# Attention probabilities and differential outputs turned by VectorE and DMA instead of TensorE

## The chip, the cores and the metric

One core of a Trainium2 chip runs the whole kernel. The metric is the device time of one execution in microseconds (us). The kernel before has a median of 2001.21 us over 3 runs (2001.2 to 2002.17). Matmuls run on TensorE (PE in the profile; PEld is its loading of the stationary operand), elementwise work on VectorE (DVE) and ScalarE (ACT). SyncE (SP) issues DMAs, and so does GpSimd (POOL), which does little else here.

## What is computed

Two transformer blocks on 256 tokens of width 2048, in float32. The first is sliding-window attention with sinks (called branch A here), 32 heads of 64:

```
scores = einsum('bnqhgd,bnkhd->bnhgqk', q, kb) * HEAD_DIM ** -0.5 - slopes * dist
p = softmax(concat([where(valid, scores, NEG), sink_col]))[..., :-1]
o = einsum('bnhgqk,bnkhd->bnqhgd', p, vb)
x = x + rmsnorm((o * silu(z)) @ w_out, g_post)
```

The second runs two attentions on the same normed input and merges them with gates, and ends with a feed-forward layer:

```
# latent branch, 16 heads of 128 + 64 rope
p = softmax(where(chunk_allowed, (qn @ kn.T + qr @ kr.T) * scale, NEG));  y_mla = p @ v
# differential branch, 8 heads, each with two maps of 128 and values of 256
a = softmax(s0) - lam * softmax(s1);  y_diff = rmsnorm_2(a @ v, sub_g) * (1 - lambda_init)
x = x + (g0 * (y_mla @ w_mla) + g1 * (y_diff @ w_diff)) @ w_out
h = rmsnorm_2(x);  x = x + (silu(h @ w_gate) * (h @ w_up)) @ w_down
out = rmsnorm_2(x)
```

With tokens in two blocks of 128, one head's probabilities are three 128x128 squares: the first query block sees one key block, the second sees two. They lie in a tile of 128 partitions (queries) by 384 columns (keys). To multiply them with the values, keys have to lie on the partitions, so each square has to be transposed.

## The kernel before

**Weights.** All weight matrices are cut on the host into 5440 tiles of 128x128, in the order in which the kernel takes them, sixteen to a chunk of 1 MB. `Weights.load` issues one DMA for a chunk on SP, into one of four `w_raw` tiles. `Weights.cut` splits half a chunk at a time into a rounded part `w_hi` (ACT, L85) and the rest `w_lo` (DVE, L86), each with four buffers; matmuls take both parts, so that their sum has float32's precision. A load waits until the chunk four before it has been cut, a cut until PE is done with the half four before it. SP's queue is in order, so whatever stands in it ahead of a load holds the load up.

**What runs between the weights.** `gemm`, `gemm_nat` and their relatives stream the weights through PE, and call `between.tiles` as they go. Every `between.every` tiles (8 or 5 in attention) that is a tick of an `Interleave`, which lets one piece of other work be written into the program there. A piece is a generator; the number that it yields is the count of ticks until its next step. In this way the attention of earlier columns stands between the weight matmuls of later ones. `attention_a` is the generator of branch A, `attend_m` that of a pair of latent heads, `attend_d` that of a differential head, `turn_residual` that of the residual after the first block.

**Turning.** `transposed` (L437) makes three PE transposes against an identity into a PSUM bank of tag `t` and copies the bank to SBUF, on DVE or ACT. In branch A the scores of pair i are followed a tick later by the transposes of pair i-1, and the values of pair i-2 stand just ahead of the scores of pair i. `attend_m` yields once before its transposes and once after them; `attend_d` transposes its probabilities at L883, splits them out of PSUM into `a_hi` and `a_lo`, multiplies, scales by the reciprocal root mean square that POOL computes (`rstd`, L280), and transposes the output at L907.

The feed-forward layers and the residual are turned in another way: DVE's `transpose` turns each 32x32 block in place, and `moved` (L449) sends the sixteen quarters, 32 partitions by 128 columns each, to where they belong, by sixteen small DMAs on POOL's queue (on SP's for two tiles of the output projection). `turn_residual` sends its eight tiles, 128 moves, on POOL.

**Memory.** Nearly all SBUF tiles are units of 128 partitions by 512 float32, in one pool of 67.

## Time and profile before

| | |
|---|---|
| median of 3 runs | 2001.21 us |
| the profiled execution | 2001.22 us, of which the span on the core is 1999.4 us |
| mean granted TensorE clock | 0.998 |
| instructions in the span | 26446 |
| read from HBM | 364.03 MB, 183 GB/s over the span |

The span is what the profile shows, from the first to the last instruction; the 1.8 us around it are in the time alone. Branch A runs from about 50 to 230 us, the latent branch from about 440 to 580, the differential heads and the residual between 600 and 1040, and the rest is merging and the feed-forward layer. Rows of groups give line, engine, operation, output and inputs, shapes, count, then busy time and mean length of one, and the engine's idle time just before them with what ended it. DVE and VectorE, ACT and ScalarE, POOL and GpSimd are the same engines; SPq and POOLq are their queues of DMA issues and waits.

### The profile page before, as it was taken

To read this page: it belongs to the slowest core of one execution; us is meant where nothing else is said; L and a number is where in the kernel's file an instruction comes from. 1 tells how busy PE (TensorE), PEld (TensorE's weight loads), DVE (VectorE), ACT (ScalarE), POOL (GpSimd) and SP (SyncE) were. 2 spreads that over 40 slices of the span, in tenths; PEclk is the share of its full clock that TensorE was granted. 3 is DMA by queue.
4 is the path that set the end of the run, shared out by engine and by line. 5 is a ranking of instruction groups with operands and counts; after the bars stand their busy time and mean duration, and the time that the engine had idled before them with its cause. 6 is when DMAs were issued, how large, how long until landed. Compare 5 with 4: busy or idle time off the path is not lost.

```text
span 1999.4 us, 26446 instructions
## 1 busy us (share of the span) xinstructions
PE 1982.0 (99%) x9956; PEld 1670.1 (84%) x9956; DVE 1231.3 (62%) x1892; ACT 1011.4 (51%) x1585; POOL 366.5 (18%) x737
## 2 busy tenths in 40 slices
PE   9999999999999999999999999999999999999997
PEld 8888888888888888888888888888888888888886
DVE  7778766977866555576565566655555555544553
ACT  6777655756545444455454344544444444434443
POOL 0000000000000542100000475533434333330000
PEclk9999999999999999999999999999999999999999
DMA  8444455444444655545555665655655655565552
GB/s 302 152 148 148 163 199 196 148 150 156 146 168 169 218 209 198 196 166 188 175 185 215 213 219 191 236 200 211 208 208 204 203 208 209 203 221 191 194 198 90
DMA packets 78512, 379.95 MB, mean 190 GB/s; under 512 B 18032, under 2 KB 30832, under 8 KB 35248
## 3 DMA queue, kind: packets, MB, share of 16 engines
q1 hardware_dynamic: 53664, 361.31, 50.8%
q0 software_dynamic: 23568, 14.99, 2.6%
q10 hardware_dynamic: 1152, 1.97, 0.3%
q8 instruction: 78, 1.28, 0.3%
q14 instruction: 50, 0.41, 0.1%
HBM read 364.03 MB, written 2.10 MB: 183 GB/s over the span
## 4 chain that ended last, share of the span: by engine, by line
PE 96%; DVE 2%; ACT 1%; issue 1%; POOL 0%; POOLq 0%; ACTq 0%
PE ps_g L199 90%; PE ps_s L199 4%; PE ps_t L199 2%; PE ps_t L441 1%; DVE rope_t L202 1%; DVE w_lo L86 0%; DVE k_n L202 0%; PE ps_warm L220 0%; DVE q_r L202 0%; ACT w_hi L85 0%; PE ps_t L907 0%; ACT prob L432 0%; PE ps_t L883 0%; DVE prob L426 0%; DVE y_m L236 0%
## 5 line engine op out<-in xcount | busy, mean ns | idle before, releaser
L86 DVE TENSOR_TENSOR w_lo<-w_raw,w_hi 128x1024 fp32r<-128x1024 f32 (+1 forms) x677 | 823.8, 1219 | 599.0 <-ACT w_hi L85 588.8
L85 ACT CAST w_hi<-w_raw 128x1024 fp32r<-128x1024 f32 (+1 forms) x677 | 710.0, 1051 | 727.0 <-PE ps_g L199 683.0
L199 PE MATMUL ps_g<-w_hi,t_hi 128*128 128x512 f32 x1176 | 457.5, 389 | 0.0
L199 PE MATMUL ps_g<-w_lo,t_hi 128*128 128x512 f32 x1176 | 457.5, 389 | 0.0
L199 PE MATMUL ps_g<-w_hi,t_lo 128*128 128x512 f32 x1176 | 457.3, 389 | 0.0
L454 POOL DMA_DIRECT2D turned<-turn x576 | 282.6, 498 | 453.8 <-DVE turn L461 251.7
L199 PE MATMUL ps_g<-h,w_hi 128*128 128x512 f32 x1160 | 284.7, 394 | 0.0
L199 PEld LDWEIGHTS ps_g<-w_lo,t_hi 128*128 128x128 f32 x1176 | 220.7, 188 | 45.9
L199 PEld LDWEIGHTS ps_g<-w_hi,t_lo 128*128 128x128 f32 x1176 | 220.7, 188 | 45.8
L199 PEld LDWEIGHTS ps_g<-w_hi,t_hi 128*128 128x128 f32 x1176 | 220.7, 188 | 45.8
L199 PEld LDWEIGHTS ps_g<-h,w_hi 128*128 128x128 f32 x1160 | 211.9, 188 | 44.1 <-issue 3.5
L199 PE MATMUL ps_g<-w_hi,h 128*128 128x512 f32 x768 | 241.3, 391 | 0.0
L199 PEld LDWEIGHTS ps_g<-w_hi,h 128*128 128x128 f32 x768 | 144.2, 188 | 29.9
L199 PE MATMUL ps_g<-h,w_lo 128*128 128x256 f32 x1160 | 156.3, 285 | 0.0
L199 PEld LDWEIGHTS ps_g<-h,w_lo 128*128 128x128 f32 x1160 | 148.9, 191 | 8.5 <-issue 3.2
L199 PE MATMUL ps_g<-w_lo,h 128*128 128x512 f32 x384 | 149.5, 389 | 0.0
L280 POOL TENSOR_TENSOR rstd<-ms,mhalf 128x2 f32<-128x2 f32 x14 | 12.4, 886 | 666.7 <-DVE ms L275 649.1
L199 PEld LDWEIGHTS ps_g<-w_lo,h 128*128 128x128 f32 x384 | 72.1, 188 | 14.7
L454 POOL DMA_DIRECT2D x1n<-turn x128 | 62.9, 499 | 103.0 <-DVE turn L936 86.7
L199 PE MATMUL ps_g<-w_hi,y_m 128*128 128x512 f32 x256 | 80.0, 390 | 0.0
L199 PE MATMUL ps_g<-w_hi,y_d 128*128 128x512 f32 x256 | 79.0, 389 | 0.0
L199 PE MATMUL ps_g<-g,w_hi 128*128 128x512 f32 (+1 forms) x240 | 57.8, 377 | 0.0
(244 smaller groups left out, 1780.5 us busy)
## 6 DMA issues: line engine op xcount, KB each, us to landing
w_raw<-w SPq DMA_DIRECT2D x337, 1024.0 KB, 4.8
turned<-turn POOLq DMA_DIRECT2D x576, 16.0 KB, 3.9
row<-rw POOLq DMA_DIRECT2D x12, 256.0 KB, 4.4
w_raw<-w SPq DMA_DIRECT2D x5, 512.0 KB, 7.5
x1n<-turn POOLq DMA_DIRECT2D x128, 16.0 KB, 3.9
x_t<-xt SPq DMA_DIRECT2D x7, 256.0 KB, 7.5
row<-rw SPq DMA_DIRECT2D x4, 256.0 KB, 6.1
out<-x1n SPq DMA_DIRECT2D x4, 256.0 KB, 3.2
```

Source lines behind the costliest of these rows:

```text
L85: a = nc.scalar.copy(out=hi[:, q], in_=src[:, q])
L86: b = nc.vector.tensor_tensor(out=lo[:, q], in0=src[:, q], in1=hi.bitcast(F32)[:, q], op=ALU.subtract)
L199: nc.tensor.matmul(out=o, lhsT=a, rhs=b, start=start, stop=stop, skip_group_check=True)
L202: nc.vector.tensor_tensor(out=o, in0=a, in1=b, op=op)
L280: nc.gpsimd.tensor_tensor(out=r, in0=t, in1=mhalf[:, 0:n], op=ALU.pow)
L441: nc.tensor.transpose(out=ps[:, j * P:j * P + P], in_=p[:, j * P:j * P + P], identity=ident)
L454: queue.dma_start(out=o[32 * b:32 * b + 32, a * P:a * P + P], in_=tr[32 * a:32 * a + 32, b * P:b * P + P])
```

## The change

Three turns go from PE to DVE and DMA.

1. The probabilities of the two heads of a pair (branch A, latent branch), or of two differential heads, are turned together by the new `turned_probs`: two DVE block transposes into a wide tile of 128 by 768 columns, then sixteen moves of 32 partitions by 192 columns, twelve on POOL's queue and four on SP's, into a second wide tile. The wide tiles come from a pool of their own with six buffers. The value matmuls read the turned tile in place, as runs of 32 columns.
2. The outputs of the differential heads are copied out of PSUM, scaled, turned by DVE (`turned_values`), moved by sixteen DMAs on POOL, and split in pieces of 128 columns. `attend_d` now takes two heads at a time, with one `rstd` for both.
3. The residual's 128 moves go from POOL's queue to SP's.

The steps stand further apart: values of branch A follow three pairs after scores instead of two, `attend_m` yields 4 and 13 ticks, `attend_d` 9 and 8. The unit pool has 57 buffers instead of 67; after the last attention the wide pool is closed, and eight units of the feed-forward activations lie in its place.

```diff
-    def transposed(p, on_act=False):
-        ps = bank("t")
-        for j in range(3):
-            nc.tensor.transpose(out=ps[:, j * P:j * P + P], in_=p[:, j * P:j * P + P], identity=ident)
...
+    def moved(tr, o, queue=nc.gpsimd, fourth=None):
+        n = tr.shape[-1] // 4
         for a in range(4):
             for b in range(4):
+                (fourth if fourth and a == 3 else queue).dma_start(
+                    out=o[32 * b:32 * b + 32, a * n:a * n + n], in_=tr[32 * a:32 * a + 32, b * n:b * n + n])
...
+    def turned_probs(p):
+        tr = wide("prob_tr")
+        o = tr.rearrange("p (b e k i) -> p e k b i", b=4, e=2, k=3)
+        for e in range(2):
+            nc.vector.transpose(out=o[:, e], in_=p[e].rearrange("p (k b i) -> p k b i", k=3, b=4))
+        d = moved(tr, wide("prob_t"), fourth=nc.sync).rearrange("p (a e k i) -> p e k a i", a=4, e=2, k=3)
+        return [d[:, e] for e in range(2)]
...
-            mm(ps[64 * e:64 * e + 64, 0:S], vs[2 * e], pts[e][:, 0:S], True, False)
+            mm(ps[64 * e:64 * e + 64, 0:S], vs[2 * e], pts[e][:, 0:2], True, False)
...
     def attention_a():
-        p, pts = {}, {}
-        for i in range(18):
+        pts = {}
+        for i in range(19):
             while i < 16 and i >= len(q_o):
                 yield
-            if i >= 2:
-                values_a(i - 2, pts.pop(i - 2))
+            if i >= 3:
+                values_a(i - 3, pts.pop(i - 3))
             if i < 16:
-                p[i] = scores_a(i)
-            yield 1
-            if 0 < i < 17:
-                a, b = p.pop(i - 1)
-                pts[i - 1] = [transposed(a), transposed(b, True)]
-            yield 2
+                p = scores_a(i)
+                yield 2
+                pts[i] = turned_probs(p)
+                yield 1
+            else:
+                yield 3
...
-        yield
-        pts = [transposed(p[e], e == 1) for e in range(2)]
-        yield
+        yield 4
+        pts = turned_probs(p)
+        yield 13
...
+    def turned_values(o, r):
+        tr = unit("o_tr")
+        to = tr.rearrange("p (b d q i) -> p q d b i", b=4, d=2, q=2)
+        for qb in range(2):
+            nc.vector.tensor_scalar(out=half(o, qb), in0=half(o, qb), scalar1=r[:, qb:qb + 1], scalar2=None,
+                                    op0=ALU.mult)
+            nc.vector.transpose(out=to[:, qb], in_=half(o, qb).rearrange("p (d b j) -> p d b j", d=2, b=4))
+        return moved(tr, unit("o_t"))
+
+    def attend_d(u, q, k, v):
+        heads = (2 * u, 2 * u + 1)
+        p = []
+        for e, head in enumerate(heads):
+            p.append(probs_d(head, q[e], k[e]))
+            yield
+        pts = turned_probs(p)
+        yield 9
+        ms = sm("ms_d")
+        os = []
+        for e in range(2):
+            os.append(values_d(pts[e], [(half(a, e), half(b, e)) for a, b in v], ms[:, 2 * e:2 * e + 2]))
+            yield
         r = rstd(ms, S)
         yield
+        ots = [turned_values(o, r[:, 2 * e:2 * e + 2]) for e, o in enumerate(os)]
+        for e, head in enumerate(heads):
+            yield 8
...
-                x1n.append(moved(tr, "x1n"))
+                x1n.append(moved(tr, unit("x1n"), nc.sync))
...
-NU = 67
+NU = 57
```

The order of PE's instructions in branch A, before, from the values of one pair through its neighbours' scores to the next transposes (`ps_t`, `ps_s`, `ps_g` are PSUM banks of the tags t, s and g; `h` numbered are parts of the normed input; rows of weight matmuls between are cut at both ends):

```order
L199 MATMUL ps_g<-h_202,w_lo 128x256
L199 MATMUL ps_t<-prob_t,v_a 64x256 x2
L199 MATMUL ps_t<-prob_t,v_a 64x128 x2
L199 MATMUL ps_s<-k_a,q_a 128x128 x2
L199 MATMUL ps_s<-k_a,q_a 128x256 x2
```

and sixteen rows of weight matmuls on:

```order
L199 MATMUL ps_g<-h_292,w_hi 128x512
L199 MATMUL ps_g<-h_321,w_hi 128x512
L199 MATMUL ps_g<-h_324,w_hi 128x512
L441 MATMUL ps_t<-ident,prob 128x128 x6
L199 MATMUL ps_g<-h_229,w_lo 128x256
L199 MATMUL ps_g<-h_232,w_lo 128x256
```

The same place of the changed kernel, with the semaphores that a row waits for in brackets (DMASW are those of POOL's DMAs, DMAHW of SP's):

```order
L209 MATMUL ps_g<-h_327,w_hi 128x512
L209 MATMUL ps_t<-prob_t,v_a 64x256 [waits DMASW6_49,DMASW5_49,DMASW7_49,DMASW4_49,DMAHW0_49,DMASW3_49,DMAHW1_49,DMASW2_49,DMAHW2_49,DMASW1_49,DMAHW7_49,DMASW0_49,PE_49]
L209 MATMUL ps_t<-prob_t,v_a 64x256
L209 MATMUL ps_t<-prob_t,v_a 64x128 x2
L209 MATMUL ps_s<-k_a,q_a 128x128 [waits DVE_49] x2
L209 MATMUL ps_s<-k_a,q_a 128x256 x2
```

The six transposes are gone, and the first value matmul of a pair waits for twelve DMA semaphores, eight of POOL's and four of SP's. On PE they take six wait instructions ahead of the matmul.

The order of SP's DMA issues before, from the start of the weight stream to the output projection (`w_raw` are the chunks):

```order
L54 DMA w_raw<-w 128x2048 x3
L515 DMA tab_a<-cst 128x384
L54 DMA w_raw<-w 128x2048 x174
L482 DMA row<-rw 128x512 x4
L54 DMA w_raw<-w 128x2048 x27
L454 DMA turned<-turn 32x128 x16
L54 DMA w_raw<-w 128x2048 x6
```

The changed kernel's, in the time of the residual and the first differential heads:

```order
L452 DMA x1n<-turn 32x128 x16
L54 DMA w_raw<-w 128x2048
L452 DMA x1n<-turn 32x128 x16
L54 DMA w_raw<-w 128x2048 x6
L452 DMA x1n<-turn 32x128 x32
L54 DMA w_raw<-w 128x2048 x7
L452 DMA x1n<-turn 32x128 x32
L54 DMA w_raw<-w 128x2048 x18
L452 DMA prob_t<-prob_tr 32x192 x4
L54 DMA w_raw<-w 128x2048 x13
```

Where 174 chunks followed each other, SP now issues moves between them: four at a time for probabilities, and the residual's in blocks of 16, twice two blocks together.

More of the change, by code (lines that the diff above doesn't have):

```diff
@@ L184, in unit, with wide, unit2 @@
         return up.tile([P, 512], dt, name=name, tag="u", bufs=NU)
+    def wide(name):
+        return wp.tile([P, 768], F32, name=name, tag="w", bufs=6)
+    def unit2(name, dt=F32):
+        return up2.tile([P, 512], dt, name=name, tag="u2", bufs=8)
     def sm(name, n=4):
@@ L461, in turned @@
         nc.vector.transpose(out=tr, in_=z)
-        return moved(tr, "turned", queue)
+        return moved(tr, unit("turned"), queue)
+    def turned_probs(p):
[5 more added lines that the diff above has]
+        return [d[:, e] for e in range(2)]
     def split_turned(acts, k0, parts):
@@ L879, in attend_d, with values_d @@
                                            in1=p[1][:, a:b], op0=ALU.mult, op1=ALU.add)
-        yield
-        ps = bank("t")
-        for j in range(3):
-            nc.tensor.transpose(out=ps[:, j * P:j * P + P], in_=p[0][:, j * P:j * P + P], identity=ident)
+        return p[0]
+    def values_d(pt, v, ms):
         ah, al = unit("a_hi", F32R)[:, 0:384], unit("a_lo", F32R)[:, 0:384]
-        nc.scalar.copy(out=ah, in_=ps[:, 0:384])
-        tt(al, ps[:, 0:384], ah.bitcast(F32), ALU.subtract)
-        yield
+        oh, ol = (o.rearrange("p (k a i) -> p k a i", k=3, a=4) for o in (ah, al))
+        nc.scalar.copy(out=oh, in_=pt)
+        tt(ol, pt, oh.bitcast(F32), ALU.subtract)
         ps = bank("t")
@@ L960, in block_kernel @@
             between.every, between.apart = 8, 3
-        for i in range(2):
-            between.add(attend_d(2 * u + i, qk[i], qk[2 + i], [(half(a, i), half(b, i)) for a, b in v]))
+        between.add(attend_d(u, qk[0:2], qk[2:4], v))
         if u == 0:
```

56 lines of the change are left out of this document (26 added, 30 removed).

## The prediction

> **What bounds the kernel now.** I read the page first: busy shares, slices, chain.
>
> ```profile
> PE 1982.0 (99%) x9956; PEld 1670.1 (84%) x9956; DVE 1231.3 (62%) x1892; ACT 1011.4 (51%) x1585; POOL 366.5 (18%) x737
> PE   9999999999999999999999999999999999999997
> PEclk9999999999999999999999999999999999999999
> PE 96%; DVE 2%; ACT 1%; issue 1%; POOL 0%; POOLq 0%; ACTq 0%
> ```
>
> PE is busy 99% of the span at the full granted clock, in every slice, and 96% of the chain that ended last is PE. So an instruction taken off PE shortens the run by its own time, as long as nothing else becomes late. Next the chain of waits in order of time, from 113 to 135 us (start, length, engine, tile, line, count), which is branch A:
>
> ```profile
> 113.92 3.88 PE ps_g L199 x16
> 117.80 0.66 PE ps_t L441 x6
> 118.46 5.56 PE ps_g L199 x32
> 124.02 0.80 PE ps_t L199 x8
> 124.82 0.85 PE ps_s L199 x8
> 125.67 2.10 PE ps_g L199 x16
> 127.78 0.66 PE ps_t L441 x6
> 128.43 5.59 PE ps_g L199 x32
> ...
> 134.02 0.80 PE ps_t L199 x8
> 134.82 0.86 PE ps_s L199 x8
> ```
>
> These pieces follow each other without a hole. Values (0.80) and scores (0.85) of a pair, weights, six transposes (0.66): two pairs take about 21.8 us (113.07 to 134.82, by the scores before and after), 10.9 a pair.
>
> **The transposes leave PE: -22.0.** The groups by form give their count:
>
> ```profile
> L441 PE MATMUL ps_t<-ident,prob 128*128 128x128 f32 x144 | 19.6, 272 | 0.6 <-DVE prob_t L446 0.6
> ...
> L907 PE MATMUL ps_t<-ident,o_d 128*128 128x128 f32 x32 | 4.8, 272 | 0.0
> ...
> L883 PE MATMUL ps_t<-ident,prob 128*128 128x128 f32 x24 | 3.9, 272 | 0.0
> ```
>
> 144 + 32 + 24 = 200. The mean of 272 ns overlaps with the next matmul; what one costs is 0.66 / 6 = 0.11 us by the chain. 200 x 0.11 = **22.0**. The other end is the busy time, 19.6 + 4.8 + 3.9 = 28.3, which counts pipeline tails; I take the chain. The 0.6 us at the end of the first row is PE waiting for a free transposing bank; it goes too: **-0.6**.
>
> [...]
>
> **Semaphores on PE: +4.3.** The order shows the first value matmul of a pair waiting for twelve DMA semaphores, where it waited for none of its own before. The built program puts them on six wait instructions in PE's queue, for 16 pairs of branch A and 8 of the latent branch (the differential heads wait on ACT and DVE instead). The one row with such an instruction on PE:
>
> ```profile
> L441 PEldq EVENT_SEMAPHORE  x10: 51/51/51, 60.4 to 560.4; - x10
> ```
>
> Six take 0.31 us at least; the time between two, no row shows. The queue may run ahead of the matmul in progress, which hides about one matmul: 3.88 / 16 = 0.24 or 2.10 / 16 = 0.13 us by the chain. That leaves 0.07 to 0.18 a pair. I take 0.18, since the six cannot take less than 0.31: 24 x 0.18 = **4.3**. Ends: 0, and 24 x 0.61 = 14.7 if each costs double and none is hidden.
>
> **DVE in branch A: +1.5.** DVE gives up a copy and gains two transposes:
>
> ```profile
> L446 DVE COPY prob_t<-ps_t 128x384 f32<-128x384 f32 x24 | 13.1, 548 | 0.4 <-PE ps_t L441 0.4
> ...
> L461 DVE STREAM_TRANSPOSE turn<-ffn 128x512 f32<-128x512 f32 x22 | 15.5, 703 | 0.0
> ...
> L936 DVE STREAM_TRANSPOSE turn<-y 128x128 f32<-128x128 f32 x32 | 8.0, 288 | 0.0
> ```
>
> 384 columns lie between: 288 + (703 - 288) x 256/384 = 565 ns. So 2 x 0.565 - 0.55 = +0.58 us a pair, plus its own wait instructions before it may overwrite a wide tile. Where gates overlap attention, DVE has little room (busy time by stretch: length, then PE, PEld, DVE, ACT, POOL):
>
> ```profile
> 150.00:200.00 50.00, 50.00 (x322) 41.38 (x320) 43.42 (x116) 38.30 (x99) 0.00 (x0) 1.00 0.43 148
> 200.00:250.00 50.00, 50.00 (x305) 42.36 (x304) 39.59 (x86) 32.68 (x72) 0.00 (x0) 1.00 0.45 164
> ```
>
> 43.42 / 50 x 10.9 = 9.5 us of DVE a pair; with 0.58 and some 0.3 of waits 10.4, and a pair now takes 10.9 - 0.66 + 0.18 = 10.4. DVE is full for five pairs. Ends 0 and 5 x 1.0; I take **1.5**. After 600 us DVE has 40% free, which hides what the differential heads add (two transposes of 565 ns and four of about 0.43 per two heads, and copies), and ACT loses its copies.
>
> **The quarters' way is hidden, and SP pays: +1.5.** POOL's moves of before (ns, least, median, most), and the DMA issues (count, size, us to landing):
>
> ```profile
> L454 POOL DMA_DIRECT2D turned<-turn x576: 496/498/550, 1119.7 to 1769.1; - x192
> ...
> w_raw<-w SPq DMA_DIRECT2D x337, 1024.0 KB, 4.8
> turned<-turn POOLq DMA_DIRECT2D x576, 16.0 KB, 3.9
> ...
> turned<-turn SPq DMA_DIRECT2D x32, 16.0 KB, 2.1
> ```
>
> And VectorE's timeline of one softmax, its first and its last step:
>
> ```profile
> 125.70 0.35 DVE L426 CUSTOM_DVE_ANT_0 prob<-ps_s,bias,negsink 128x128 f32<-128x128 f32 x1 [1.15 <-PE ps_s L199]
> ...
> 129.39 0.62 DVE L566 TENSOR_SCALAR prob<-prob,rec 128x256 f32<-128x256 f32 x2
> ```
>
> A pair's probabilities are ready at 130.0, 5.2 us after its scores (124.82). Then 1.1 of transposes, 12 x 0.498 = 6.0 of issue on POOL, 3.9 to land: 16.2 us. Values now come three pairs after scores, 3 x 10.4 = 31 us. SP's four moves can stand behind a weight load by one load interval (5.4): 8 us of cover stay. The latent branch waits 13 ticks of 5 weight tiles, the differential one 9 of 8, both above 20 us. If that cover were gone, PE would idle by each us, 24 times. So 0 here. The last heads' 32 moves take 16 + 3.9 us of the 8 ticks (22 us) that they have.
>
> SP also takes the residual's 128 moves, two times 32 in a row with no load between them, by the order. Rows for that: SP's timeline, PE's chain over the same time, and the two halves of a cut:
>
> ```profile
> 1228.15 10.96 SPq L54 DMA_DIRECT2D w_raw<-w  x3
> 1242.18 10.10 SPq L454 DMA_DIRECT2D turned<-turn  x16
> 1252.37 19.59 SPq L54 DMA_DIRECT2D w_raw<-w  x6
> ...
> 1037.82 943.88 PE ps_g L199 x4164
> ...
> L86 DVE TENSOR_TENSOR w_lo<-w_raw,w_hi 128x1024 fp32r<-128x1024 f32 (+1 forms) x677 | 823.8, 1219 | 599.0 <-ACT w_hi L85 588.8
> L85 ACT CAST w_hi<-w_raw 128x1024 fp32r<-128x1024 f32 (+1 forms) x677 | 710.0, 1051 | 727.0 <-PE ps_g L199 683.0
> ```
>
> Sixteen moves hold SP for 10.2 us; PE did not stop. A chunk is 24 matmuls of 943.88 / 4164 = 0.227, so 5.44 us. At a load's issue three chunks lie uncut (16.3) and four halves are cut (10.9, less 1.05 + 1.22 of cutting): PE needs the new chunk 24.9 us later. It needs 4.8 to land and 2.3 to be cut, so it can be 17.8 late; loads may lie 5.44 + 17.8 = 23.2 apart. A block of 32 makes that 20.4 + 0.4 + w, w being SP's wait for the turn before it: 3.1 in the rows above (1239.1 to 1242.2). Over by 0.6; w lies between 0 and 5.4, so a block costs 0 to 3.0: twice 0.6 to 0.8, **+1.5**, ends 0 and 6. Fewer units (57 for 67) I cost at nothing: PE's chain has no hole from 1038 to 1982 us, where most units are held.
>
> **Sum**: -22.0 - 0.6 + 4.3 + 1.5 + 1.5 = -15.3. The profiled execution took 2001.22 (span 1999.4), the median of the runs is 2001.21: forecast **1985.9**.
>
> **Rivals.** *Everything hidden*: waits, DVE and SP all have cover; 2001.2 - 22.6 = 1978.6. For it: PE shows no holes even at 87% DVE. Against: six times 51 ns exceed the matmul ahead. *POOL becomes the bound in branch A, slower than before*: at p us per move a pair costs POOL 12p. At 0.498 that is 6 of 10.4 us, and 704 moves show at most 0.55, but none of them ran beside a DVE as full as here. Beyond p = 0.87 quarters fall behind by 12p - 10.4 a pair, less the 8 us of cover once: the gain of 15.3 is gone at (12p - 10.4) x 16 = 23.3, p = 0.99; at 1.1 the time is 1985.9 + 36.8 = 2023. [...] *Strided reading*: the value matmuls now read their moving operand in runs of 32 numbers, which no matmul of before does. If it halves their speed, 24 x 0.80 = 19.2 comes back: 2005. *It doesn't do what it says*: PE's rows go, yet late weights or evictions give all of it back, 2000.
>
> **Chances.** Forecast (1982 to 1991) 0.50; everything hidden (below 1982) 0.27; one cover partly gone, waits at double price (1991 to 1997) 0.09; no net change 0.06; slower, by POOL or the strides, 0.08. The range goes from 1976, the hidden case with some of the 28.3, to 1997, forecast plus the upper end of the semaphores. 0.2%, about what a measurement of this kernel can tell from no change, is 4 us: faster 0.86, same 0.06, slower 0.08.
>
> **What would show it.** No rows with ident in branch A; PE busy some 20 us less; value matmuls still 0.80 a pair with up to 0.2 idle before them, put down to DMA; DVE near 95% between 150 and 200 us; idle on PE of about a us after each block of 32 on SP, between 690 and 780 us; POOL moves at 0.5. I am wrong if value groups take 1.2 or more, if POOL's mean rises past 0.9, or if PE waits over 3 us in one place.

## The result, and the profile after

The changed kernel has a median of 1983.32 us over four executions (1981.54 to 1986.96), the kernel before beside it 2001.54 (2001.2 to 2002.17). The ratio is 0.9911, with a 95% interval of 0.9894 to 0.9928. The profiled execution took 1981.54 us, 19.7 less than the 2001.22 of before. The forecast was 1985.9.

From the page of the changed kernel, busy time by engine (time, share of the span, instructions) and TensorE's row of the 40 slices:

```profile
PE 1960.2 (99%) x9756; PEld 1648.5 (83%) x9756; DVE 1247.0 (63%) x1960; ACT 997.5 (50%) x1577; POOL 526.9 (27%) x1069
PE   9999999999999999999999999999999999999998
```

PE has 200 matmuls less and is busy for 21.8 us less. It is still what bounds the kernel. POOL gained 160 us and DVE 16, and neither shows at this scale.

TensorE's timeline in branch A of the changed kernel (start, length, operation, shapes, count), from the values of one pair to those of the next:

```profile
119.24 0.87 PE L209 MATMUL ps_t<-prob_t,v_a 128*64 128x256 f32 x8
120.05 0.93 PE L209 MATMUL ps_s<-k_a,q_a 64*128 64x128 f32 x8
120.90 2.17 PE L209 MATMUL ps_g<-h,w_lo 128*128 128x256 f32 x16
122.91 3.82 PE L209 MATMUL ps_g<-h,w_hi 128*128 128x512 f32 x16
126.57 2.07 PE L209 MATMUL ps_g<-h,w_lo 128*128 128x256 f32 x16
128.57 0.87 PE L209 MATMUL ps_t<-prob_t,v_a 128*64 128x256 f32 x8
```

Each piece begins where the one before it ends, but for the overlap in the pipeline: values begin 0.81 us before the scores, as before (0.80), with no idle time in brackets ahead of them although the first of them follows six wait instructions. The six transposes are gone, and nothing stands in their place.

Busy time by stretch, where gates and attention overlap (stretch, then its length, PE, PEld, DVE, ACT, POOL, granted clock, DMA share, GB/s):

```profile
150.00:200.00 50.00, 50.00 (x309) 41.17 (x308) 45.58 (x129) 38.96 (x106) 26.96 (x56) 1.00 0.57 187
```

DVE rose from 43.42 to 45.58 us of 50, that is 91%, and PE lost nothing there. The new work itself, from the groups (VectorE's turns), the view of one tile (POOL's moves: least, median, most, in ns) and the DMA issues (size, us to landing):

```profile
L467 DVE STREAM_TRANSPOSE prob_tr<-prob 128x384 f32<-128x384 f32 x56 | 30.7, 565 | 0.3
```

```profile
L452 POOL DMA_DIRECT2D prob_t<-prob_tr x336: 496/496/667, 55.9 to 1016.5; - x168
```

```profile
prob_t<-prob_tr POOLq DMA_DIRECT2D x336, 24.0 KB, 3.6
```

A turn takes the 565 ns that lay between the two sizes of before, and a move on POOL 0.5 us beside a DVE that is 91% busy. The value matmuls that read in runs of 32, from the groups by form of both kernels, the changed one first:

```profile
L209 PE MATMUL ps_t<-prob_t,v_a 128*64 128x256 f32 x64 | 10.4, 405 | 0.0
```

```profile
L199 PE MATMUL ps_t<-prob_t,v_a 128*64 128x256 f32 x64 | 10.4, 404 | 0.0
```

Where the gain is given back is in TensorE's waits (for what, us in total, times, longest):

```profile
PE ps_g L209 <- ACT w_hi L85: 3.4, 3, 2.2
PE ps_g L209 <- DVE w_lo L86: 1.5, 2, 0.8
```

The waits of before have no such rows. By time they are 2.2 us at 777 us, 0.7 at 1023 and 1.4 at 1366; the 0.6 left of the first row lies at 6 us, in the start.

Idle time understates what such a stall costs: a weight matmul's row is 0.39 us long while the next one starts 0.23 us after it, and idle is counted from the end of the row. The whole cost, called the delay from here on, comes out by laying two traces side by side, since the n-th matmul into `ps_g` has the same operands and shapes in every kernel of this case (8792 in each trace). Against the kernel before, the changed one falls back by 0.45 us at 739 us, where no wait of 0.2 us stands, by 2.5 at 777, 1.0 at 1023 and 1.9 at 1366: 5.9 us in all, where the waits say 4.3.

The stall at 777, in SyncE's timeline (start, length, count) and TensorE's:

```profile
695.60 13.49 SPq L54 DMA_DIRECT2D w_raw<-w  x6
710.62 20.88 SPq L452 DMA_DIRECT2D x1n<-turn  x32
731.60 15.57 SPq L54 DMA_DIRECT2D w_raw<-w  x7
751.68 21.50 SPq L452 DMA_DIRECT2D x1n<-turn  x32
773.28 26.16 SPq L54 DMA_DIRECT2D w_raw<-w  x9
```

```profile
775.23 2.00 PE L209 MATMUL ps_g<-h,w_hi 128*128 128x512 f32 x8
779.47 0.73 PE L209 MATMUL ps_g<-h,w_hi 128*128 128x512 f32 x2 [2.24 <-ACT w_hi L85]
```

The second block of 32 moves begins 4.5 us after the last load ahead of it was issued (747.17 to 751.68), since SP waits for its turn, and then takes 21.5. PE stops 2.24 us, and the load behind the block is what ACT waited for. The first block, 1.5 us after its load and 20.9 long, is the delay of 0.45.

### How the executions are compared

The time alone does not tell a microsecond, and so each profile is also read at a mark near the end: the start of SyncE's four last output moves. Before, and after:

```profile
1984.64 6.25 SPq L1090 DMA_DIRECT2D out<-x1n  x4
```

```profile
1967.31 6.18 SPq L1126 DMA_DIRECT2D out<-x1n  x4
```

The mark comes 17.3 us earlier, the end of the span 19.6 (1999.4 to 1979.8). What follows the mark takes 14.8 us in the one profile and 12.5 in the other; in the profiles below it lies between 11.1 and 14.1, and does not go with any edit. So 17.3 is what the change did in these two executions, and some 2.3 us is the end.

### The profile page after: what moved, and what is told of

Read it like the earlier page. It is cut to its first block, busy times and chain, and to the rows that moved or that the text cites. A ratio compares the mean times of both kernels' runs of the same rounds, so it can differ in the third digit from the quotient of the medians.

```text
span 1979.8 us, 27202 instructions
## 1 busy us (share of the span) xinstructions
PE 1960.2 (99%) x9756; PEld 1648.5 (83%) x9756; DVE 1247.0 (63%) x1960; ACT 997.5 (50%) x1577; POOL 526.9 (27%) x1069
## 5 line engine op out<-in xcount | busy, mean ns | idle before, releaser
L452 POOL DMA_DIRECT2D prob_t<-prob_tr x336 | 164.7, 498 | 397.5 <-DVE prob_tr L467 274.2
L290 POOL TENSOR_TENSOR rstd<-ms,mhalf 128x2 f32<-128x2 f32 (+1 forms) x10 | 9.2, 920 | 358.6 <-DVE ms L285 341.0
L209 PEld LDWEIGHTS ps_g<-w_lo,h 128*128 128x128 f32 x384 | 72.1, 188 | 16.2 <-DVE w_lo L86 1.6
L452 POOL DMA_DIRECT2D o_t<-o_tr x128 | 62.8, 498 | 63.0 <-issue 24.8
```

What stands on the lines that cost most here:

```text
L209: nc.tensor.matmul(out=o, lhsT=a, rhs=b, start=start, stop=stop, skip_group_check=True)
L290: nc.gpsimd.tensor_tensor(out=r, in0=t, in1=mhalf[:, 0:n], op=ALU.pow)
L452: (fourth if fourth and a == 3 else queue).dma_start(out=o[32 * b:32 * b + 32, a * n:a * n + n], in_=tr[32 * a:32 * a + 32, b * n:b * n + n])
```

## The experiments

All kernels ran beside the kernel before (medians 2001.39 to 2002.11). The table has the medians of four or five executions (eleven for the kernel before with its moves on SP), their range, the ratio to the kernel before and its 95% interval, the profiled time and the mark.

| kernel | median, us | range | ratio | profiled | mark |
|---|---|---|---|---|---|
| changed | 1983.32 | 1981.54 to 1986.96 | 0.9911 [0.9894, 0.9928] | 1981.54 | 1967.31 |
| residual's moves on POOL | 1977.64 | 1976.99 to 1978.46 | 0.9880 [0.9865, 0.9895] | 1978.46 | 1963.58 |
| 13 ticks for 9 | 1982.52 | 1981.37 to 1983.04 | 0.9902 [0.9886, 0.9919] | 1983.04 | 1968.41 |
| t_hi in program order | 1981.27 | 1979.36 to 1983.61 | 0.9898 [0.9883, 0.9913] | 1983.61 | 1969.31 |
| the three edits | 1977.15 | 1976.40 to 1980.11 | 0.9880 [0.9865, 0.9895] | 1977.61 | 1962.58 |
| three, four waits on PE | 1982.40 | 1978.48 to 1984.13 | 0.9901 [0.9888, 0.9915] | 1983.81 | 1969.62 |
| three, eight waits on PE | 1977.82 | 1977.25 to 1979.08 | 0.9882 [0.9869, 0.9896] | 1978.31 | 1962.65 |
| three, values two behind | 1991.76 | 1989.82 to 1994.91 | 0.9955 [0.9943, 0.9968] | 1991.70 | 1976.79 |
| before, moves on SP | 2002.66 | 2002.17 to 2003.63 | 1.0005 [0.9996, 1.0014] | 2003.31 | 1987.40 |
| residual's moves on both | 1976.68 | 1975.80 to 1978.74 | 0.9874 [0.9859, 0.9889] | 1978.74 | 1965.77 |
| three, differential as before | 1981.53 | 1981.15 to 1982.57 | 0.9901 [0.9887, 0.9914] | 1982.57 | 1969.68 |
| three, pairs as before | 1991.63 | 1991.22 to 1992.50 | 0.9951 [0.9939, 0.9964] | 1991.63 | 1978.68 |
| three, moves on both | 1976.45 | 1974.47 to 1976.69 | 0.9871 [0.9855, 0.9888] | 1976.21 | 1963.22 |

The theory from the changed kernel's profile was that the transposes bring all of their own time, that nothing on PE pays for the semaphores, and that three late places, each with a cause of its own, give some of it back. The first three kernels after the changed one in the table take one cause each, the fourth takes all.

**The residual's moves.**

```diff
-                x1n.append(moved(tr, unit("x1n"), nc.sync))
+                x1n.append(moved(tr, unit("x1n")))
```

> The changed kernel, with the residual's 128 moves issued by POOL instead of SP. Theory SP: two blocks of 32 moves on SP hold back weight loads, and the second one makes PE wait 2.4 us at 776.8 us, the 11.1 us of ACT idle for w_raw there being the trace of it. Then that stall goes, no ACT idle for w_raw above 3 us is left between 690 and 790 us, and the profiled execution comes out 2 to 3 us below that of the changed kernel (1981.5), at 1978.5 to 1979.5; the stalls at 1023 (0.9) and 1366 (1.8) stay. The repeats, which lie between 1981.5 and 1987.0 for the changed kernel, come closer together if what differs among them is how far the loads behind a block are late. Rival: the loads at 777 are late from the memory's side, or POOL, which now has 128 moves more of about 0.5 us, brings the quarters of the differential heads later and ACT waits longer at a_hi: then PE idles as much in another place, and the time stays at 1981.5 to 1984.

The stall at 777 us went, and ACT waits 3.5 us for `w_raw` in the whole run, at most 2.5 at a time (31.8 and 11.1 in the changed kernel). The mark is 3.7 us earlier, more than the 2.2 of that stall, since the one at 1366 us, which was expected to stay, is absent here as well; 0.5 near 1022 stays. It would be 1.0 earlier still, but in this execution PE ran at half its clock from 332.8 to 336.2 us, as it did in half of the profiles (last section). The median is 5.7 us lower. This edit alone brings most of what there was to get.

**The wait before the differential values.**

```diff
         pts = turned_probs(p)
-        yield 9
+        yield 13
```

> The changed kernel, with 13 ticks instead of 9 between the turning of the differential heads' probabilities and their use. Theory ACT: at 1013.8 to 1021.7 us ACT stands 7.9 us at the first a_hi of the last two heads, since twelve of their sixteen moves stand on POOL behind 32 moves of the heads before; cuts of weights queue behind a_hi on ACT, and PE waits 0.9 us at 1023.3. With 13 ticks a_hi stands six weight halves (16 us) later in ACT's order, so the 7.9 us and the 0.9 us go, and nothing else changes: 0.9 us less than the changed kernel (1980.6 in the profiled execution). Rival: those ticks only shift the wait to the outputs' moves, or to the end of the branch, where the last y_d is needed by PE (12 halves, 33 us later): the time stays or grows by up to 4 us with PE waiting for y_d before 1050 us.

The place in ScalarE's timeline of the changed kernel, where the brackets give the idle time before a row, and in that of this kernel:

```profile
1012.71 1.05 ACT L85 CAST w_hi<-w_raw 128x1024 fp32r<-128x1024 f32 x1 [0.50 <-PE ps_g L209]
1021.68 0.51 ACT L894 CAST a_hi<-prob_t 128x384 fp32r<-128x384 f32 x1 [7.91 <-DMA row<-rw]
1022.10 2.94 ACT L85 CAST w_hi<-w_raw 128x1024 fp32r<-128x1024 f32 x3
```

```profile
1033.68 0.50 ACT L894 CAST a_hi<-prob_t 128x384 fp32r<-128x384 f32 x1
```

ACT stood for 7.91 us: three cuts that PE needed came in its order behind one copy that waited for quarters, and began at 1022.10 us, 0.42 after that copy had started. (The `row` named is the last DMA on POOL's queue before it, not what the copy reads.) With 13 ticks ACT does not wait there, and PE has no stall near 1023. The profiled execution is nevertheless no shorter: the ticks also moved the residual's turns, a block of 32 now stands at 618 us with loads 24.4 us apart, and PE waits 2.3 us there, and 1.7 at 1366. The delays are 2.8 and 3.9, for behind the second of these the clock stood at half for 3.4 us. So the step is shown, and its gain can't be seen in the time by itself.

**The order on ScalarE in the feed-forward layer.** The first two parts of the feed-forward output write their `t_hi` into the eight units that lie in the wide pool's place. The order of ACT's instructions there, before and in the changed kernel (a count behind x; shapes left out, the last row cut):

```
before                                        changed
L1024 ACTIVATE ffn<-ps_g,r x2                 L1060 ACTIVATE ffn<-ps_g,r x2
L85 CAST w_hi<-w_raw x10                      L85 CAST w_hi<-w_raw x7
L1024 ACTIVATE ffn<-ps_g,r x2                 L480 CAST t_hi<-turned
L85 CAST w_hi<-w_raw                          L85 CAST w_hi<-w_raw x3
L472 CAST t_hi<-turned                        L480 CAST t_hi<-turned
L85 CAST w_hi<-w_raw                          L1060 ACTIVATE ffn<-ps_g,r x2
L472 CAST t_hi<-turned                        L85 CAST w_hi<-w_raw x13
```

The ticks ahead of these copies are as before. They stand four and two halves earlier. A likely reason is that their tiles, from a pool of their own, are free at once; no run tests that by itself. The edit holds them where the program writes them:

```diff
-            nc.scalar.copy(out=oh, in_=t)
+            c = nc.scalar.copy(out=oh, in_=t)
+            if make is unit2:
+                pin(c)
```

> The changed kernel, with the copies t_hi of the first eight k of the ffn's output kept in program order on ACT, so that they stand there as in the kernel before (t_hi after 17 halves and an evict, not 12 to 15). Theory units: the separate pool of eight units made these tiles free at once, the scheduler put t_hi 3 to 4 halves earlier than before, ACT waits there 5.2, 6.6 and 5.7 us for moved quarters, and PE loses 0.74 + 1.03 us at 1366 us behind the second part. Then both stalls go, ACT's idle for turned falls from 34.4 us to about the 17.0 of before, and the profiled execution is 1.8 us shorter than that of the changed kernel: 1979.7. Rival: these stalls come from late loads (SP's issue of w_raw) and not from ACT's order: they stay, 1981.5.

ScalarE's waits of the changed kernel and of this one:

```profile
ACT t_hi L480 <- DMA turned<-turn: 34.4, 9, 6.6
```

```profile
ACT t_hi L480 <- DMA turned<-turn: 17.8, 7, 5.2
```

The wait falls to that of before (17.0), and the stall at 1366 is gone. The order alone does not make that stall: with the residual's moves on POOL the copies stand as early as in the changed kernel, but the two in question wait 2.0 and 5.0 us there instead of 6.6 and 5.7, and PE does not stop. The profiled time is longer than the changed kernel's all the same, since in this execution both blocks of 32 made PE wait, 1.9 us at 740 and 1.5 at 782. The delays are 4.0, of which 1.7 is the clock at half behind the stall, and 1.8.

**The three edits together.**

> The three edits together. If the three stalls have the three causes named, all go and the gains add: 1981.5 - 2.4 - 0.9 - 1.8 = 1976.4 in the profiled execution, PE busy above 99.9% in every stretch of 50 us between 700 and 1950 us, and repeats within 2 us of each other. This is also the time of a change whose every added wait is hidden: 2001.2 less 22.0 of transposes less 0.6 and 1 to 2 of stalls that went in the latent branch. If the semaphore waits on PE cost 0.18 us each as I had put it, the time cannot go below about 1980.9 (1976.6 + 4.3). Rival: the lost time appears elsewhere, since ACT and POOL are as full as before: 1979 to 1984.

```profile
1962.58 6.31 SPq L1128 DMA_DIRECT2D out<-x1n  x4
```

No wait of PE for `w_hi` or `w_lo` is left among the waits of this profile. The mark is 4.7 us earlier than in the changed kernel, which had 2.2 + 0.7 + 1.4 = 4.3 us of these stalls, and 22.1 us earlier than before. It holds 1.0 us of half clock at 333 us, which the profiles of the kernel before and of the changed one do not have; without it the gain is 23.1: the 22.0 of the transposes, the 0.6 at the transposing bank, and a wait of 0.4 for `negmax` at 516 us that is also gone. The same 1.0 is most of the 1.2 by which the profiled 1977.6 lies above the expected 1976.4. One repeat took 1980.11, and that is not explained.

**The semaphores.** The three edits, with all sixteen moves of a pair on POOL, or half of them on SP. PE's wait instructions ahead of the first value matmul are then four or eight for six; the traces have 171 wait rows of PE at the line of the matmuls with six, 120 with four and 220 with eight, where two for each of 24 pairs make 48 (the first line of the edit is cut at its end):

```diff
-        d = moved(tr, wide("prob_t"), fourth=nc.sync)
+        d = moved(tr, wide("prob_t"))
```

```diff
-                (fourth if fourth and a == 3 else queue).dma_start(
+                (fourth if fourth and a >= 2 else queue).dma_start(
```

> The kernel of the three edits, with all sixteen moves of a pair's probabilities on POOL. The first value matmul of each of 24 pairs then has four wait instructions ahead of it on PE instead of six. Theory hidden: PE's queue runs ahead of its matmuls far enough that these waits cost nothing; then the time stays at that of the three edits (1977.6 profiled, 1977.15 median) within its spread, as long as POOL's 8.0 us per pair fit into the 10.2 us of a pair. Rival, as I had priced it: n instructions cost n x 51 ns less 0.13 us, so 0.07 instead of 0.18 us a pair: 24 x 0.10 = 2.4 us less, 1975.2, and the time from the first to the last score of branch A falls by 16 x 0.10 = 1.6 us. A second rival: POOL becomes late, quarters land after 28 us, and PE waits before value matmuls.

> The kernel of the three edits, with eight of a pair's sixteen moves on SP and eight on POOL: eight wait instructions ahead of each of 24 first value matmuls on PE instead of six. Theory hidden: no change on PE, 1977.6 profiled, and the time from the first to the last score of branch A is the same to 0.3 us with four, six and eight waits. Rival, as priced: 0.28 instead of 0.18 us a pair, 24 x 0.10 = 2.4 us more, 1980.0, 1.6 us of it in branch A. A second way to get longer: SP's eight moves (5.1 us) now stand in a load interval of 5.4 us and weights come late, which ACT's idle for w_raw would show.

TensorE's first and last scores of branch A, with no waits ahead of the values (before), with six (three edits) and with eight:

```profile
48.18 0.92 PE L199 MATMUL ps_s<-k_a,q_a 64*128 64x128 f32 x4
...
211.76 0.93 PE L199 MATMUL ps_s<-k_a,q_a 64*128 64x128 f32 x8
```

```profile
48.43 0.92 PE L209 MATMUL ps_s<-k_a,q_a 64*128 64x128 f32 x4
...
201.88 0.93 PE L209 MATMUL ps_s<-k_a,q_a 64*128 64x128 f32 x8
```

```profile
48.52 0.92 PE L209 MATMUL ps_s<-k_a,q_a 64*128 64x128 f32 x4
...
201.96 0.93 PE L209 MATMUL ps_s<-k_a,q_a 64*128 64x128 f32 x8
```

163.58 us before, and 153.45, 153.44 and, with four, 153.45 (48.16 to 201.61): the same to 0.01 us. A wait instruction on PE costs nothing here, and the trace shows why. The waits of the pair whose values start at 119.39 us with six, and at 119.48 with eight (count, ns, first and last start):

```profile
L209 PEldq EVENT_SEMAPHORE  x6: 51/51/51, 115.4 to 116.0; - x6
```

```profile
L209 PEldq EVENT_SEMAPHORE  x8: 51/51/51, 115.5 to 116.3; - x8
```

They follow each other at 0.1 us, so six take 0.64 us rather than 0.31. But they are over more than 3 us before the matmul starts, beside matmuls that are still running; in every second pair the lead is smaller, and with eight the last wait still starts 1.7 us ahead.

The 10.1 us that went are 15 intervals of a pair, 0.675 each, the 0.66 of six transposes. With four waits another rival came true behind that stretch: with all moves on POOL the quarters of the last two pairs landed some 31 us after their scores, and PE waited for them:

```profile
PE ps_t L209 <- DMA prob_t<-prob_tr: 2.3, 1, 2.3
...
PE ps_t L209 <- issue: 1.3, 1, 1.3
```

POOL's moves stay at 0.5 us, but now it also waits between them for earlier ones to land (44 times, 49 us in all, against 13 times, 12.6 us, with twelve moves a pair). A load of `lam` for another branch, on the same queue, went out at 140.4 us instead of 132.9, and DVE stood for it in its own order:

```profile
143.42 0.42 DVE L212 TENSOR_TENSOR lam<-lam 128x256 f32<-128x256 f32 x1 [5.81 <-DMA lam<-bc]
```

From there on the turns come 10 to 14.4 us after the scores, where with six waits they come 5.2 to 9.6 after. Another 1.3 us of waits for weights at 967 us are in this profile too.

**The cover.** The three edits, with values two pairs behind their scores:

```diff
-        for i in range(19):
+        for i in range(18):
...
-            if i >= 3:
-                values_a(i - 3, pts.pop(i - 3))
+            if i >= 2:
+                values_a(i - 2, pts.pop(i - 2))
```

> The kernel of the three edits, with the values of branch A two pairs behind the scores instead of three. In the profile of the three edits POOL ends its moves 12.3 to 13.8 us after the scores in ten of sixteen pairs, and 14.6 to 19.8 in six, and they land 3.6 later; values come 27.2 to 30.7 after the scores, two pairs behind they would come after about 18 to 20.5. Theory cover: the way of the quarters is what it costs beside a full DVE, 16 us in the pairs without gates and up to 23.4 with them; three pairs behind, all is hidden; two behind, PE waits in the late pairs alone (3.4 us at the eleventh, up to 1 at two others): 3 to 6 us more than the three edits, 1980 to 1984, with PE's waits put down to prob_t's DMAs between 150 and 210 us. Rival: POOL's late moves are late because the tiles they write are still read by the values three pairs behind; these come free a pair earlier now, the way shrinks with them, and PE loses less than 1 us.

```profile
PE ps_t L209 <- DMA prob_t<-prob_tr: 6.4, 3, 2.5
PE ps_t L209 <- issue: 2.9, 1, 2.9
```

Both guesses were too low: the mark is 14.2 us later, and 15.3 were lost in branch A, since the 1.0 at 333 us is absent here. Four pairs of the second half wait, 9.3 us in all. Their turns come 8.4 to 11 us after the scores where the others' come after 5.1 to 6.3, with the gates' work on DVE ahead of them, and the quarters land after 20 us and more. The rival, by which the way would shrink with the distance, is out: POOL's last move of the eleventh pair ends 21.4 us after the scores here, 19.8 with three pairs. The rest is mostly the clock, in the stretches around the first of these stalls (last three columns: granted clock, DMA share, GB/s):

```profile
149.00:153.00 4.00, 1.09 (x11) 0.92 (x11) 3.48 (x6) 1.42 (x4) 3.75 (x8) 0.89 0.93 285
153.00:155.00 2.00, 2.00 (x12) 1.36 (x14) 1.08 (x3) 0.86 (x3) 2.00 (x5) 0.50 0.86 356
155.00:157.00 2.00, 2.00 (x10) 1.20 (x7) 0.76 (x4) 0.34 (x1) 0.15 (x1) 0.50 0.58 221
```

Behind the stall PE runs at half its clock for 6.8 us, from 152.2 to 159.0, so that 2.9 us of idle cost 5.7.

**The blocks on SP by themselves.** The kernel before, with its residual's moves on SP:

```diff
-                x1n.append(moved(tr, "x1n"))
+                x1n.append(moved(tr, "x1n", nc.sync))
```

> The kernel before, with nothing changed but the queue of the residual's 128 moves: SP instead of POOL, in blocks of 32, 16, 16, 32, 16 and 16 without a load between the moves of a block. Theory SP: the loads behind a block of 32 come too late by 0 to 3 us each, with what SP waits for the turn; PE has the same work as before: 2001.8 + 2 to 6 = 2004 to 2008, repeats over a range of 3 us or more (1.0 us in the kernel before), ACT idle for w_raw of 8 us or more once or twice between 690 and 800 us, and PE waiting for w_hi behind it. Rival: the 5.7 us that the residual's moves on POOL gave to the changed kernel (1983.3 to 1977.6) came of SP's probabilities, which stand among the same loads, together with those blocks; alone the blocks cost less than 1 us: 2001.4 to 2002.8.

SyncE's and TensorE's timelines of this kernel around its first block of 32:

```profile
645.54 0.33 SPq L54 DMA_DIRECT2D w_raw<-w  x1
650.42 20.21 SPq L454 DMA_DIRECT2D x1n<-turn  x32
670.74 8.91 SPq L54 DMA_DIRECT2D w_raw<-w  x5
```

```profile
676.95 0.50 PE L199 MATMUL ps_g<-w_hi,h 128*128 128x512 f32 x1 [0.24 <-ACT w_hi L85]
678.21 0.50 PE L199 MATMUL ps_g<-w_lo,h 128*128 128x512 f32 x1 [0.76 <-DVE w_lo L86]
```

The loads on the two sides of the block start 25.2 us apart, and PE waits 1.0 us, a delay of 1.6; the second block, 22.1 apart, costs nothing. (The mark is 2.8 later than before, of which 1.0 is the clock at 343 us.) The median rises by 1.3 us, inside the interval of no change and below the 2 to 6 expected, and the repeats range over 1.5 us, not 3. The mechanism is there without the change; its size of 5.7 us is not.

Then the moves of the changed kernel, half on each queue:

```diff
+                (fourth if fourth and a == 3 else half_on if half_on and a >= 2 else queue).dma_start(
...
+                x1n.append(moved(tr, unit("x1n"), half_on=nc.sync))
```

> The changed kernel, with eight of the residual's sixteen moves a turn on SP and eight on POOL: SP's blocks are 8, 8, 8, 8, 16 and 16 moves long instead of 16, 16, 16, 16, 32 and 32. Theory block: a stall needs two loads of weights to lie more than about 23 us apart; so far gaps of 22.8, 22.1 us cost 0 to 0.3 us and gaps of 24.4 to 26.4 cost 1.4 to 2.7. A block of 16 takes 10.2 us and leaves gaps of 16 us at most: no PE wait for w_hi between 600 and 800 us, and a median as with all moves on POOL, 1977.6 (1977 to 1979). Rival: any move on SP among the loads costs, in proportion to their number, as it waits there for DVE and makes loads late: half of the 5.7 us is left, 1980.5.

No two loads around these blocks are more than 15.0 us apart (746.5 to 761.5), PE does not wait for weights between 600 and 800, and the median is as low as with POOL alone. So it is the length of a block that counts, not that SP issues the moves. The blocks of 32 in all profiles:

| loads apart, us | kernel | PE's waits, us | delay, us |
|---|---|---|---|
| 22.1 | before, moves on SP | none | 0 |
| 22.8 | changed | none | 0.45 |
| 23.1 | t_hi in order | 1.9 | 4.0 |
| 24.4 | 13 ticks | 2.3 | 2.8 |
| 25.2 | before, moves on SP | 1.0 | 1.6 |
| 25.7 | t_hi in order | 1.5 | 1.8 |
| 26.4 | changed | 2.2 | 2.5 |

Below 23 us next to nothing is lost; above it the loss does not grow with the gap. The profile of this kernel has stalls of 1.0 at 1020, 0.8 at 1269 and 0.8 at 1366 us, behind ACT's waits for quarters.

**The parts by themselves.** The three edits, with the code of before for the differential heads (`attend_d`), or with that of before for the pairs of branch A and of the latent branch (`transposed`, `values_a`, `attention_a`, `attend_m`).

> The kernel of the three edits with the differential heads as before, probabilities and outputs transposed by PE (56 of the 200 transposes), branch A and the latent branch as changed. Theory: PE's own time alone counts, 56 x 0.11 = 6.2 us more: 1983.8 profiled (1977.6 with the three edits), median 1983.3. Rival: the differential part gives its gain back in waits of its own (ACT at a_hi and y_d, POOL's 32 moves in a row, DVE's extra 2.5 us a head pair), so that undoing it costs less than 2 us: 1977 to 1979.

> The kernel of the three edits with branch A and the latent branch as before, their probabilities transposed by PE (144 of the 200 transposes), the differential heads as changed. Theory: 144 x 0.11 = 15.8 us more, and the stalls at a transposing bank that the kernel before has (0.6 by the chain, 0.5 to 0.8 at two places of the latent branch) are back: 1977.6 + 15.8 + 0.6 to 1.9 = 1994.0 to 1995.3. Rival: the wide turns cost branch A and the latent branch something that their traces do not show as a wait (twelve more semaphores, reads in runs of 32 numbers): then undoing them costs less than 14 us, below 1992.

The marks of the two:

```profile
1969.68 6.23 SPq L1102 DMA_DIRECT2D out<-x1n  x4
```

```profile
1978.68 6.30 SPq L1140 DMA_DIRECT2D out<-x1n  x4
```

Undoing the differential part moves the mark by 7.1 us, of which 0.9 is the delay of a stall at 1197 us (0.5 in the waits): 6.2, as 56 x 0.11. Undoing the other moves it by 16.1. It has no half clock at 333 us, so 17.1 are to be explained: 15.8, the wait of 0.6 at a transposing bank and that of 0.4 for `negmax`, which are back, to 0.3. By the times both came out below the expected: the medians moved by 4.4 and 14.5, and the second kernel's 1991.63 lies below the 1992 that its rival had named. That speaks at most weakly for the rival, since in both profiles only 11.1 and 11.2 us follow the mark, against 13.2 with the three edits; the marks agree with the theory.

**The best version.** The three edits and the moves on both queues:

> The kernel of the three edits with the residual's moves half on SP and half on POOL, as in x1n_half, whose profile left PE 1.4 us idle at 1020 us (behind ACT's 8.4 us at a_hi), 1.3 at 1269 and 0.9 at 1366 (behind ACT's waits for moved quarters in the ffn). Theory order: those at 1020 and 1366 come of where a_hi and t_hi stand in ACT's order, so the ticks and the pin remove them here too, while that at 1269, whose t_hi no edit moves, may stay: SP's last four output moves begin at 1962.6 to 1964 us, as with the three edits (1962.58; x1n_half 1965.77), and the median is 1975 to 1976.7. Rival: ACT's waits follow from how POOL's moves collide, so they only change places: PE idles 2 us or more between 1000 and 1400 us again, and the median stays at 1976.7 or above.

The mark, 1963.22, lies where it was expected; the stalls at 1020 and 1366 are gone, 0.8 us stays at 1269 and 0.3 at 1188 (delays 1.2 and 0.6). Its median of 1976.45 is 6.9 us below the changed kernel and 25.7 below the kernel before beside it (2002.11). Against the three edits alone it is not to be told apart.

## Why the prediction was right, and where not

**Transposes, -22.0: right.** 200 x 0.11 is what the marks show in parts and together, once the 0.6 at the transposing bank, the 0.4 for `negmax` and the 1.0 of half clock at 333 us are counted: 6.2 of 6.2, 16.1 of 15.8 and 23.1 of 22.0 + 0.6 + 0.4. The 0.6 went too, and came back with the transposes; the 0.4 was not in the sum.

**Semaphores, +4.3: mis-sized, 0.** The step that failed is "the queue may run ahead of the matmul in progress, which hides about one matmul". Four, six and eight instructions gave the same 153.45 us. The six take 0.64 us, twice what I had as the least, but the queue is 2.4 to 4.0 us ahead of the matmul when the first of them starts, many matmuls and not one. The lower end, 0, was the value; I had taken 0.18 a pair because six could not hide behind one matmul.

**DVE in branch A, +1.5: mis-sized, 0.** DVE is at 91%, not 95, and PE stays at 50.00 of 50 us. But the step's fear was sound: with one pair less of distance, turns held up by the gates cost 15 us.

**SP, +1.5: right in kind, too small in size, 3.0 in this profile.** The limit worked out from rows, loads 23.2 us apart, is where stalls begin (22.8 costs 0.45, 23.1 is the first with a wait in the rows). The wait w was 1.5 and 4.5 us, not twice 3.1, so one block cost next to nothing and the other nearly all. In other executions both cost: 5.9 us in the profile of the t_hi kernel, with the clock at half behind one of them, and the median falls by 5.7 when the moves leave SP, near the upper end of 6. The sum priced a late load at its lateness alone; a stall that is followed by a slower clock cost more (2.9 us of idle cost 5.7 with values two behind), and no term had that.

**The quarters' way, at nothing: right in branch A, not in the differential heads.** In the eleventh pair of the three edits POOL's last move ends 19.8 us after the scores and lands 3.6 later, values come at 30.7: 7.3 us of cover at the narrowest. That this is near the predicted 8 is luck: the way was 23.4 us, not 16.2, since DVE turned this pair late, and the numbers given for the 8 (31, 16.2 and 5.4) leave 9.4. For the differential heads I compared 9 ticks with the way of one pair's moves alone; at the last heads POOL first issued 32 moves of outputs. The wait fell on ACT, where cuts of weights stood behind it, and PE lost 1.0 us.

**Units, at nothing: wrong, 1.9.** The step that failed is to take PE's chain without a hole after 1038 us as a sign that nothing there could come late. What the runs show is an order: two copies stood earlier on ACT, in front of DMAs that had not landed, and holding them in program order removed the stall. That the pool of their own moved them is likely and was not tested by itself.

**Sum.** Expected at the mark: -15.3. Found: -17.3. Without any stall the gain by the matmuls is 23.3, 0.7 more than the 22.6 that the sum had for the transposes and their bank, and the delays of 5.9 (3.0 on SP, 1.0 at 1023, 1.9 at 1366) come off it. So the near total is in part luck: 5.8 us priced for semaphores and DVE were not paid, and 4.4 us were paid that had been priced at nothing or too low. The further 2.3 us of the profiled time came after the mark, by chance as far as the other profiles tell. The median of 1983.32 is 2.6 us below the forecast. The rival "everything hidden" (1978.6) did not come true in the changed kernel, but it is the three edits, 1977.6. Of the others, POOL's moves stayed at 0.5 us (496 ns at the median, 667 at most), beside a DVE that is 91% busy, and reading in runs of 32 costs nothing (405 and 404 ns).

What stays open: how the 5.7 us between the medians with and without the moves on SP divide. The delays behind the blocks are 3.0 us in one profile and 5.9 in another, and the stall at 1366, 1.9 in the changed kernel, also came and went, so sums of that size do occur; but only one execution of each kernel was profiled.

## What to carry to other kernels

Where one engine bounds the whole span, as PE does here (99% busy), work taken off it counts in full (23.1 us found at the mark with the three edits, of 23.0), and the pricing should go to the queues that the new work passes through: ask of each in-order queue (loads on SP, cuts on ACT) what now stands ahead of what the bound engine needs. A block of small DMAs in a queue of loads cost next to nothing here (0 to 0.45 us) as long as the loads on its two sides began less than 23 us apart, where PE takes a chunk every 5.4, and 1.6 to 4.0 us beyond; rows gave that limit ahead of the runs (23.2), so work it out and break the block below it. A change can reorder an engine that it never mentions, as ACT's copies of the feed-forward layer here, so the new order of every in-order engine is to be read, not only of those with new work.

## What the hardware showed that was not expected

**PE's clock stood at half behind some short idles.** The stalls of 2.9, 2.55 and 2.03 us (values two behind), one of 2.3 (four waits), one of 1.9 (t_hi kernel, at 741) and one of 1.7 (13 ticks, at 1367) were followed by a granted clock of 0.50. Those of 1.8 (values two behind), 1.5 (t_hi kernel, at 783) and 1.3 (four waits), the 2.24 at 777 of the changed kernel and the 2.3 at 646 with 13 ticks, were followed by 1.00. The shortest case stands in every kernel: 0.64 us of idle between 332 and 348 us, behind matmuls of 128x1 and 128x128, was followed by half clock in seven of the fourteen profiles, the three edits among them. There, and in the changed kernel, where it was not:

```profile
332.40 0.70 PE L209 MATMUL ps_t<-diag,ones 128*128 128x256 f32 x2 [0.64 <-DVE diag L297]
332.75 3.58 PE L209 MATMUL ps_s<-g 128*128 128x512 f32 x8
```

```profile
332.25 0.70 PE L209 MATMUL ps_t<-diag,ones 128*128 128x256 f32 x2 [0.64 <-DVE diag L297]
332.60 2.20 PE L209 MATMUL ps_s<-g 128*128 128x512 f32 x8
```

So the length of the idle does not decide alone. The clock records of the traces show a grid: every slow stretch amid the work lasted 3.41 us, or twice that once, and began a whole multiple of 3.41 us after the first full clock of its execution (327.68 us, which is 96 of them, with the three edits). With values two behind, the slow stretches begin at 152.2, 179.5 and 203.4 us, eight and then seven of them apart. At the end, where PE has no more work, the full clock ends 1983.14 us after its start before and 1969.49 in the changed kernel, 581 and 577 times 3.4133. Cut along that grid, every stretch of 3.41 us with 1.87 us of idle or more was followed by half clock (five cases). Of those with 1.5 to 1.82 one was (1.67) and three were not, and of those with less only that place and, with values two behind, the stretch from 152.2 us, which had 0.8 us of idle and was slow itself. The 2.24 us at 777 fell on both sides of a border (779.0), with 1.80 on one of them. Why 0.64 us was followed by half clock there is open. With the three edits the small matmuls just before it and the idle (331.8 to 332.4) lie in one stretch, 329.4 to 332.8; in the changed kernel a border, at 331.9, falls amid the idle (331.6 to 332.25). No run tested whether that is the cause.

**Eight wait instructions ahead of a matmul cost PE nothing here.** In a row, 0.1 us apart, they changed nothing in 153 us (153.44 with eight, 153.45 with four and six), as they ran 1.7 us and more ahead of the matmul that they guard.

**The end of the span varies.** From the last output moves of SP to the last instruction it took 11.1 to 14.8 us with nothing changed there, more than several of the edits are worth.
